# Output projection and second norm in token halves, two feed-forward operands placed between, output tiles that keep their slots

## The chip, the core and the metric

The kernel runs on one core of one Trainium2 chip. The metric is the device time of one execution in microseconds (us). Below, TensorE is the matrix engine (PE in the views, PEld its weight loads), VectorE is DVE, ScalarE is ACT, GpSimd is POOL, and SyncE (SP) issues the DMAs.

## The reference, cut to what matters

One layer of a streaming encoder for 1024 tokens of width 1024, in float32:

```
h   = rmsnorm(x, ln1)
mix = concat(pool_mixer, gla_mixer, forgetting_attention)(h @ w_in)   # 256 + 256 + 512 columns
x3  = x + mix @ w_o
h2  = rmsnorm(x3, ln2)
x4  = x3 + (silu(h2 @ w_gate) * (h2 @ w_up)) @ w_down                 # D_FF = 2816
out = rmsnorm(x4, ln_f)
```

The forgetting attention has eight heads of 64. It is causal, so a block of 256 queries m (0 to 3) looks at m + 1 blocks of 256 keys.

## The kernel before, in words

**Number format.** Each float32 operand is split into a high part (a copy into the matrix format, by ACT) and a low part (the difference, by VectorE or POOL). A product of two matrices is three matrix products: high x high, high x low, low x high.

**Stages.** Norm and projections; pooling and gated linear attention; four pairs of attention heads p = 0..3; output projection with the residual; second norm; gate and up projection (22 tiles fi of 128 columns); down projection; last norm. The feed-forward matrix products are done by a seven-product scheme on halves (products 1 to 7, in the order 3, 5, 4, 1, 2, 7, 6). So each needs operands that are sums of halves, split again into high and low.

**Output projection.** The mixed columns come as eight tiles mix0 to mix7 of 128 channels. `out_proj` makes a block tb of 128 tokens from four of them: first from mix0 to mix3 (PSUM name pxa), later from mix4 to mix7 (pxb), 24 products each, in two column halves; VectorE adds each to the residual tile xa (L576). Mix tiles are held in two groups g of 512 tokens. mix4 to mix6 are read back from DRAM as mr (L560), split by ACT (L562) and POOL (L563). mix7 is written in place by the last attention pair (`last_mix`). Before, group g holds the 256-token blocks g and g + 2, since tokens m * 256 go to `last_mix[m % 2]`. The last pair does its query blocks m in the order 3, 1, 2, 0, and pxb, x3d and the norm run over the blocks in the order 2, 3, 6, 7, 0, 1, 4, 5.

**Second norm.** For each block: ACT squares (L632), VectorE and POOL make the reciprocal root (n_v, n_r, L100 and L101), VectorE scales (L634), TensorE transposes (n2pt, L639), ACT copies to hr (L641). `left(i)` makes the left operand hA of product i from hr: a sum hs by VectorE where two halves are needed (L667), high by ACT (L670), low by VectorE (L671). hr0 and hr1 hold tokens 0 to 511, hr2 and hr3 tokens 512 to 1023. `right(fi)` loads wg and wu (L681, L682) and makes seven right operands: sum ws (L693; by POOL for the first two tiles), high (L694), low (L695). `gate_up` does the products m (L710).

**Slots.** SBUF is cut into 50 tiles of 128 x 1024 float32. `G` takes the first tile of a list `idle`, `free` puts one at its end, so that a new tile waits for whatever last used its slot. `ws` and some others come from a ring of two half tiles. PSUM has four tags: s (3 banks), pt (2), o (1), gm (2).

**Down projection.** `prep` makes the operands of two column tiles at a time: ra is loaded (L803), rw summed by POOL (L808), both split (L815 ACT, L816 VectorE) to ha, la, hw, lw. The last index is that of the first of the two tiles: rw6_10 is product 6, tile 10, a single one. The products d are at L916, their adds into the output tiles c at L894 and L896. `final(tb)` scales c (L883, L884), stores it to `out` and frees its slot.

**Order of instructions.** The program is written in the order of the functions, but a scheduler arranges the instructions of each engine by its own estimate of time. What an engine does in which order is therefore fixed when the kernel is built, and each engine works strictly in that order. So an edit in one place can move instructions in others.

Of the kernel before, what the change touches and what calls it, by code (L numbers as in the profile page):

```python
# [10 lines left out]
F32R = mybir.dt.float32r  # L11
I8 = mybir.dt.int8
AF = mybir.ActivationFunctionType
ALU = mybir.AluOpType
# [4 lines left out]
P = 128  # L19
NT = T // P  # L20
# [11 lines left out]
def tile_hybrid_block(ctx: ExitStack, tc, x, w_fv, w_gv, w_zt, w_o, w_gu, w_down, ln, w_pool, w_a3, chans, b_f, consts, out):  # L32
    nc = tc.nc
    ACT, DVE, POOL, PE, SP = nc.scalar, nc.vector, nc.gpsimd, nc.tensor, nc.sync
# [8 lines left out]
    idle = list(range(NSLOT))  # L43
    where = {}
    rings, n_ = {}, NSLOT
# [4 lines left out]
    def G(name, dtype=F32):  # L50
        i = idle.pop(0)
        t_ = big.tile([P, 1024], dtype, tag=f"g{i}", name=name)
        where[name] = i
        return t_

    def free(*names):
        for n in names:
            idle.append(where.pop(n))
# [10 lines left out]
    def f(ap):  # L69
        return ap.bitcast(F32)  # L70
# [181 lines left out]
    last_mix = []  # L252
# [205 lines left out]
    def fox_item(p, a, m, ops, fb, V):  # L458
# [6 lines left out]
        for i in range(2):  # L465
# [3 lines left out]
            w = W // nh  # L469
# [59 lines left out]
        if p < 3:  # L529
            SP.dma_start(mixd[4 + p, rows, m * 256:(m + 1) * 256], oy[rows])  # L530
        else:
            hi, lo = (last_mix[m % 2][rows, h, (m // 2) * 256:(m // 2 + 1) * 256] for h in range(2))
            ACT.activation(hi, oy[rows], AF.Copy)
            POOL.tensor_tensor(out=lo, in0=oy[rows], in1=f(hi), op=ALU.subtract)

    def fox_attend(p, ops, V):
        fbs = []
        for a in range(2):
            fb = R(f"fb{p}_{a}", tag="fb")
            SP.dma_start(fb, Fd[2 * p + a:2 * p + a + 1, :].broadcast_to([P, T]))  # L540
            fbs.append(fb)
        for a, m in ([(a, m) for a in range(2) for m in range(4)] if p < 3 else [(a, m) for m in (3, 1, 2, 0) for a in range(2)]):
            fox_item(p, a, m, ops, fbs[a], V)


# [2 lines left out]
    def load_mix(k0, g):  # L548

        mixes = []  # L550
        for k in range(k0, k0 + 4):
            if k == 7:
                mixes.append(last_mix[g])
                free(f"mr6_{g}")
                break
            if k % 2 == 0:
                raw = G(f"mr{k}_{g}").rearrange("p (k c t) -> p k c t", k=2, c=2)
            t_ = G(f"mix{k}_{g}", F32R).rearrange("p (h t) -> p h t", h=2)
            src = raw[:, k % 2]
            SP.dma_start(src, mixd[k].rearrange("p (c g t) -> p c g t", c=2, g=2)[:, :, g])  # L560
            hi, lo = (t_[:, h].rearrange("p (c t) -> p c t", c=2) for h in range(2))
            ACT.activation(hi, src, AF.Copy)  # L562
            POOL.tensor_tensor(out=lo, in0=src, in1=f(hi), op=ALU.subtract)  # L563
            mixes.append(t_)
            if k % 2:
                free(f"mr{k - 1}_{g}")
        return mixes

    def out_proj(tb, x2, mixes, ws, name):

        o0 = (tb // 4) * 256 + (tb % 2) * P
        for nh in range(2):
            ns = slice(nh * 512, nh * 512 + 512)
            ps = PS("gm", f"{name}{tb}_{nh}")
            gemm(ps, [((t_[:, 0, o0:o0 + P], t_[:, 1, o0:o0 + P]), (wh[:, ns], wl[:, ns])) for t_, (wh, wl) in zip(mixes, ws)])
            DVE.tensor_tensor(out=x2[:, ns], in0=ps, in1=x2[:, ns], op=ALU.add)  # L576
# [33 lines left out]
    xs = {}  # L610
    for g in range(2):
        mixes = load_mix(0, g)
        for tb in (2 * g, 2 * g + 1, 2 * g + 4, 2 * g + 5):
            xs[tb] = G(f"xa{tb}")
            SP.dma_start(xs[tb], x[tb * P:(tb + 1) * P, :])
            out_proj(tb, xs[tb], mixes, ws, "pxa")
        free(*[f"mix{k}_{g}" for k in range(4)])
# [11 lines left out]
    def norm2(tb, x2):  # L629
        ss = S(f"n2ss{tb}")  # L630
        sq = G(f"n2sq{tb}")
        ACT.activation(sq, x2, AF.Square, scale=D ** -0.5, accum_out=ss)  # L632
        r = rstd_D(ss, 1, f"n2{tb}")
        DVE.scalar_tensor_tensor(out=sq, in0=x2, scalar=r[:, 0:1], in1=ln2, op0=ALU.mult, op1=ALU.mult)  # L634
        o = slice((tb % 4) * P, (tb % 4) * P + P)
        for half in range(2):
            pt = PS("pt", f"n2pt{tb}_{half}")
            for k in range(4):
                PE.transpose(pt[:, k * P:(k + 1) * P], sq[:, (4 * half + k) * P:(4 * half + k + 1) * P], ident)  # L639
            for kp in range(2):  # L640
                ACT.activation(raw[2 * (tb // 4) + half][kp][:, :, o],  # L641
                               pt[:, 2 * kp * P:(2 * kp + 2) * P].rearrange("p (k t) -> p k t", k=2), AF.Copy)
        free(f"n2sq{tb}")

    mixes = [load_mix(4, g) for g in (1, 0)][::-1]
    for tb in (2, 3, 6, 7, 0, 1, 4, 5):
        g = (tb // 2) % 2
        out_proj(tb, xs[tb], mixes[g], ws, "pxb")
        SP.dma_start(x3d[tb], xs[tb])
        norm2(tb, xs[tb])  # L650
        free(f"xa{tb}")
        if tb in (7, 5):
            free(*[f"mix{k}_{g}" for k in range(4, 8)])
    free("wo6h", "wo6l", "wo7h", "wo7l", "ln2b")
    idle.extend(rings.pop("wr") + rings.pop("w"))


    hA = {}

    def left(i, in0, in1=None, op=None):  # L660
        hA[i] = []
        for kp in range(2):
            hi, lo = (G(f"hA{i}_{kp}{h}", F32R).rearrange("p (k t) -> p k t", k=2) for h in "hl")
            src = raw[in0][kp]
            if in1 is not None:
                t_ = G(f"hs{i}{kp}").rearrange("p (k t) -> p k t", k=2)
                DVE.tensor_tensor(out=t_, in0=src, in1=raw[in1][kp], op=op)  # L667
                src = t_
                free(f"hs{i}{kp}")
            ACT.activation(hi, src, AF.Copy)  # L670
            DVE.tensor_tensor(out=lo, in0=src, in1=f(hi), op=ALU.subtract)  # L671
            hA[i].append((hi, lo))


    cd = dpool.tile([7, NF // 2, P, 512], F32, name="cd")
# [114 lines left out]
    def prep(count):  # L790
        for i, j0, nj in items[len(ready):count]:
# [30 lines left out]
                    free(f"wd0_{j}", f"wd1_{j}")  # L822
            ready.append(ops)

    seen = []

    def start(fi):
        w_ = right(fi)

        def done(i):  # L830
            free(f"wr{fi}_{i}")
            if fi == NF - 1:
# [6 lines left out]

    lefts = {1: (0, 3, ALU.add), 4: (3,), 2: (2, 3, ALU.add), 3: (0,), 5: (0, 1, ALU.add), 7: (1, 3, ALU.subtract),  # L840
             6: (2, 0, ALU.subtract)}
    first = [start(fi) for fi in range(2)]
    for i in (3, 5, 4, 1, 2, 7, 6):
        left(i, *lefts[i])
        if i == 7:
            free("hr1_0", "hr1_1", "hr3_0", "hr3_1")
        for g_ in first:
            next(g_)
# [31 lines left out]
    def final(tb):  # L880
        x2 = cx[tb]
        r = rstd_D(sums[tb], 2, f"f{tb}")
        DVE.scalar_tensor_tensor(out=x2[:, 512:], in0=x2[:, 512:], scalar=r[:, 0:1], in1=lnf[:, 512:], op0=ALU.mult, op1=ALU.mult)  # L883
        ACT.activation(x2[:, 0:512], x2[:, 0:512], AF.Copy, scale=r[:, 0:1])  # L884
        for nh in (1, 0):
            ns = slice(nh * 512, nh * 512 + 512)
            SP.dma_start(out[tb * P:(tb + 1) * P, ns], x2[:, ns])
        free(f"c{tb}")

    def add_down(i, t, bank):  # L890
        for th, nh, sign in DEST[i]:
# [117 lines left out]
```

## Time and profile before

| | us |
|---|---|
| median of three runs | 1199.56 |
| lowest and highest | 1198.48, 1200.44 |
| profiled execution, its own time | 1203.56 |
| span of the profiled execution (first to last instruction) | 1201.8 |
| TensorE busy in the span | 1159.9 (97%) |
| VectorE busy | 810.2 (67%) |
| ACT busy | 530.9 (44%) |
| POOL busy | 390.9 (33%) |
| mean granted clock of TensorE | 0.979 |

Stages as the trace of before has them: last attention pair about 400 to 495 us, pxa beside it from 404 to 492, pxb and the second norm 498 to 561, gate and up 553 to 977, down projection 977 to 1195, last norm to 1201.8.

How to read the rows in the prediction. A row of the timeline has start, duration, engine, source line, operation, out<-in tile names, shape, and in brackets the idle time of the engine before it with what ended that. A row of a window has for each engine the busy time and the number of instructions, then the granted clock (PEclk), the share of the DMA engines, and GB/s. A row of the groups has the count, the busy time and the mean of one in ns, then idle time before. A row of the waits has the waiting operation, the one that released it, and us in total, times, longest. A row of the DMA issues has count, KB each, and the us from issue to landing. Line numbers are those of the kernel before. In the kernel after, the feed-forward functions stand above the pxb loop, so their lines differ: ws L664, high and low L665 and L666, m L681, rw L779, d L922.

### The profile page before, as it was taken

The numbers are of one execution on the slowest core, as the hardware profiler recorded it, in microseconds if no ns is written. First come the engines' busy times: TensorE is split into PE (matmuls) and PEld (weight loads), VectorE is DVE, ScalarE is ACT, GpSimd is POOL, SyncE is SP. The second block draws the span as 40 slices with busy tenths as digits, with TensorE's granted clock in tenths as the row PEclk, the third lists the DMA queues.
The fourth block names the chain that finished last, engine by engine and source line by source line (L and its number), as shares of the span: only waits on it lengthen the run. The fifth ranks groups of instructions, "written<-read, shape, count | busy, mean of one in ns | idle before, by whom it ended". The sixth has DMA issues, their size and how long they took to land.

```text
span 1201.8 us, 15933 instructions
## 1 busy us (share of the span) xinstructions
PE 1159.9 (97%) x5928; PEld 974.8 (81%) x5928; DVE 810.2 (67%) x1328; ACT 530.9 (44%) x965; POOL 390.9 (33%) x285
## 2 busy tenths in 40 slices
PE   6999999999999989899999999999999999999995
PEld 6878788889988778777888888888888888888874
DVE  7567612278748676468998768676776685766674
ACT  6362121257656745346444334443343344334353
POOL 2163122243333823331022220122202270660873
PEclk9999889899999999899999999999999999999998
DMA  6121111111122522221153331323224588333223
GB/s 244 35 71 53 54 35 53 36 55 47 47 62 77 169 91 97 79 105 53 53 155 112 111 120 65 131 93 118 95 90 148 214 322 288 109 96 118 63 97 140
DMA packets 53565, 126.34 MB, mean 105 GB/s; under 512 B 4792, under 2 KB 10344, under 8 KB 53488
## 3 DMA queue, kind: packets, MB, share of 16 engines
q1 hardware_dynamic: 53056, 123.75, 30.7%
q0 software_dynamic: 432, 1.57, 0.4%
q8 instruction: 46, 0.75, 0.3%
q14 instruction: 31, 0.25, 0.1%
HBM read 93.03 MB, written 32.28 MB: 104 GB/s over the span
## 4 chain that ended last, share of the span: by engine, by line
PE 84%; DVE 5%; DMA 3%; issue 3%; POOL 3%; ACT 2%; POOLq 0%; SPq 0%; ACTq 0%; DVEq 0%
PE m L710 35%; PE d L916 16%; PE pxa L138 4%; PE psv L138 3%; PE o L524 3%; PE pt L510 2%; PE s L484 1%; PE zq0p L138 1%; PE zgg0p L138 1%; PE s L485 1%; DMA mr<-mixd 1%; PE psg L138 1%; PE po L364 1%; PE zq3p L138 1%; PE zgg1p L138 1%
## 5 line engine op out<-in xcount | busy, mean ns | idle before, releaser
L710 PE MATMUL m<-hA_0h,wr 128*128 128x512 f32 x616 | 214.3, 390 | 0.6 <-ACT hr L641 0.5
L710 PE MATMUL m<-hA_1h,wr 128*128 128x512 f32 x616 | 214.6, 389 | 0.0
L710 PEld LDWEIGHTS m<-hA_0h,wr 128*128 128x128 f32 x616 | 115.6, 188 | 24.9 <-ACT hr L641 1.1
L710 PEld LDWEIGHTS m<-hA_1h,wr 128*128 128x128 f32 x616 | 115.7, 188 | 23.9
L916 PE MATMUL d<-hw,ha 128*128 128x512 f32 x308 | 120.0, 392 | 5.3 <-ACT hw L815 5.3
L710 PE MATMUL m<-hA_0l,wr 128*128 128x512 f32 x308 | 119.9, 389 | 1.7 <-DVE hA_0l L671 1.7
L916 PE MATMUL d<-lw,ha 128*128 128x512 f32 x308 | 120.4, 391 | 0.8 <-DVE lw L816 0.8
L710 PE MATMUL m<-hA_1l,wr 128*128 128x512 f32 x308 | 119.8, 389 | 0.0
L762 POOL TENSOR_TENSOR cg<-cu,cu 128x512 f32<-128x512 f32 x11 | 19.2, 1742 | 308.7 <-DVE cu L739 308.7
L916 PE MATMUL d<-hw,la 128*128 128x512 f32 x308 | 118.8, 391 | 0.0
L694 ACT ACTIVATE wr<-ws 128x512 fp32r<-128x512 f32 x110 | 69.5, 631 | 109.2 <-DVE ws L693 54.9
L695 DVE TENSOR_TENSOR wr<-ws,wr 128x512 fp32r<-128x512 f32 x110 | 75.9, 696 | 26.0 <-ACT wr L694 26.0
L816 DVE TENSOR_TENSOR la<-ra,ha 128x1024 fp32r<-128x1024 f32 (+1 forms) x42 | 58.2, 1392 | 29.0 <-ACT ha L815 21.5
L808 POOL TENSOR_TENSOR rw<-wd,wd 128x512 f32<-128x512 f32 x33 | 56.4, 1737 | 51.3 <-PE d L916 46.6
L916 PEld LDWEIGHTS d<-hw,ha 128*128 128x128 f32 x308 | 58.1, 189 | 17.8 <-ACT hw L815 5.7
L710 PEld LDWEIGHTS m<-hA_0l,wr 128*128 128x128 f32 x308 | 57.8, 188 | 14.2 <-DVE hA_0l L671 2.2
L916 PEld LDWEIGHTS d<-lw,ha 128*128 128x128 f32 x308 | 58.3, 189 | 13.3 <-DVE lw L816 1.2
L815 ACT ACTIVATE ha<-ra 128x1024 fp32r<-128x1024 f32 (+1 forms) x42 | 41.2, 987 | 61.6 <-DMA ra<-cd 56.0
L916 PEld LDWEIGHTS d<-hw,la 128*128 128x128 f32 x308 | 58.1, 189 | 12.1
L710 PEld LDWEIGHTS m<-hA_1l,wr 128*128 128x128 f32 x308 | 57.8, 188 | 12.1
L499 POOL TENSOR_TENSOR pb<-pb,rl 128x128 f32<-128x128 f32 (+3 forms) x32 | 38.1, 1196 | 83.4 <-DVE rl L496 66.5
L816 DVE TENSOR_TENSOR lw<-rw,hw 128x1024 fp32r<-128x1024 f32 (+1 forms) x30 | 45.7, 1535 | 27.3 <-ACT hw L815 27.2
(391 smaller groups left out, 2764.1 us busy)
## 6 DMA issues: line engine op xcount, KB each, us to landing
ra<-cd SPq DMA_DIRECT2D x35, 512.0 KB, 3.7
wu<-in_w_gu_dram SPq DMA_DIRECT2D x22, 512.0 KB, 4.3
wg<-in_w_gu_dram SPq DMA_DIRECT2D x22, 512.0 KB, 3.7
wd<-in_w_down_dram SPq DMA_DIRECT2D x22, 512.0 KB, 6.5
cd<-cg SPq DMA_DIRECT2D x11, 512.0 KB, 4.6
cd<-cs SPq DMA_DIRECT2D x11, 512.0 KB, 6.2
cd<-cu SPq DMA_DIRECT2D x11, 512.0 KB, 7.5
fb<-Fd SPq DMA_DIRECT2D x8, 512.0 KB, 4.5
```

Of the source, the lines that this page charges most:

```text
L138: PE.matmul(ps, a, b, start=(n == 0), stop=(n == last))
L499: POOL.tensor_tensor(out=pb[:, 0:W], in0=pb[:, 0:W], in1=rl[:, 0:1].broadcast_to([P, W]), op=ALU.mult)
L510: PE.transpose(pt[:, o0:o0 + P], Pb[i][:, (2 * n + b) * P:(2 * n + b + 1) * P], ident)
L524: PE.matmul(*args, start=(kb == 0 and n_ == 0), stop=(last and n_ == 1))
L694: ACT.activation(hi, src, AF.Copy)
L695: e2.tensor_tensor(out=lo, in0=src, in1=f(hi), op=ALU.subtract)
L710: PE.matmul(ps, a, b, start=(n == 0), stop=(n == 11))
L762: POOL.tensor_tensor(out=t_[:, 0:512], in0=a11, in1=a12, op=ALU.add)
L808: POOL.tensor_tensor(out=raw_[:, j * 512:j * 512 + 512], in0=wd[h0, j0 + j][:, e0, :], in1=wd[h1, j0 + j][:, e1, :], op=op)
L815: ACT.activation(hi[:, sl], src, AF.Copy)
L816: DVE.tensor_tensor(out=lo[:, sl], in0=src, in1=f(hi[:, sl]), op=ALU.subtract)
L916: PE.matmul(banks[t], a[:, o], b[:, ns], start=(j0 + j == 0 and m == 0), stop=(j0 + j == NF // 2 - 1 and m == 2))
```

## The change

- The last attention pair does its blocks m in the order 1, 0, 3, 2, and a group g holds the token half g (blocks 2g and 2g + 1). So a group's mr is loaded as one piece of 512 tokens.
- pxa, pxb, the stores x3d and the second norm run over tb = 0 to 7.
- Group 1 of mix4 to mix7 is asked for at tb = 2, and not ahead of the loop.
- At tb = 4, when tokens 0 to 511 are normed, the left operands of products 3 and 5 and the right operands of tile 0 are written; those of tile 1 follow behind the loop. For that the feed-forward functions stand ahead of the loop.
- `final` does not free the slot of c.

The core of the diff (the functions moved are the same text):

```diff
-            hi, lo = (last_mix[m % 2][rows, h, (m // 2) * 256:(m // 2 + 1) * 256] for h in range(2))
+            hi, lo = (last_mix[m // 2][rows, h, (m % 2) * 256:(m % 2 + 1) * 256] for h in range(2))
...
-        for a, m in ([(a, m) for a in range(2) for m in range(4)] if p < 3 else [(a, m) for m in (3, 1, 2, 0) for a in range(2)]):
+        for a, m in ([(a, m) for a in range(2) for m in range(4)] if p < 3 else [(a, m) for m in (1, 0, 3, 2) for a in range(2)]):
...
-                raw = G(f"mr{k}_{g}").rearrange("p (k c t) -> p k c t", k=2, c=2)
+                raw = G(f"mr{k}_{g}").rearrange("p (k t) -> p k t", k=2)
...
-            SP.dma_start(src, mixd[k].rearrange("p (c g t) -> p c g t", c=2, g=2)[:, :, g])
+            SP.dma_start(src, mixd[k, :, g * 512:(g + 1) * 512])
...
-        o0 = (tb // 4) * 256 + (tb % 2) * P
+        o0 = (tb % 4) * P
...
-        for tb in (2 * g, 2 * g + 1, 2 * g + 4, 2 * g + 5):
+        for tb in range(4 * g, 4 * g + 4):
...
-    mixes = [load_mix(4, g) for g in (1, 0)][::-1]
-    for tb in (2, 3, 6, 7, 0, 1, 4, 5):
-        g = (tb // 2) % 2
-        out_proj(tb, xs[tb], mixes[g], ws, "pxb")
-        SP.dma_start(x3d[tb], xs[tb])
-        norm2(tb, xs[tb])
-        free(f"xa{tb}")
-        if tb in (7, 5):
-            free(*[f"mix{k}_{g}" for k in range(4, 8)])
-    free("wo6h", "wo6l", "wo7h", "wo7l", "ln2b")
...
-    first = [start(fi) for fi in range(2)]
+    mixes = [load_mix(4, 0), None]
+    first = []
+    for tb in range(NT):
+        if tb == 2:
+            mixes[1] = load_mix(4, 1)
+        if tb == 4:
+            free(*[f"mix{k}_0" for k in range(4, 8)])
+            for i in (3, 5):
+                left(i, *lefts[i])
+            first.append(start(0))
+        out_proj(tb, xs[tb], mixes[tb // 4], ws, "pxb")
+        SP.dma_start(x3d[tb], xs[tb])
+        norm2(tb, xs[tb])
+        free(f"xa{tb}")
+    free("wo6h", "wo6l", "wo7h", "wo7l", "ln2b", *[f"mix{k}_1" for k in range(4, 8)])
+    idle.extend(rings.pop("wr") + rings.pop("w"))
+    first.append(start(1))
     for i in (3, 5, 4, 1, 2, 7, 6):
-        left(i, *lefts[i])
+        if i not in (3, 5):
+            left(i, *lefts[i])
...
-        free(f"c{tb}")
```

What the scheduler makes of it is seen in the order of each engine. First POOL near the end of the program, before: rw6_2 to rw6_10 are sums for the last products, c0 to c3 (L878) output tiles that are multiplied by the norm's weight, f0_r to f3_r their reciprocal roots.

```order
L808 TENSOR_TENSOR rw6_4_10183<-wd0_5_8906,wd1_5_8638 128x512
L808 TENSOR_TENSOR rw6_2_10102<-wd0_2_8847,wd1_2_8617 128x512
L808 TENSOR_TENSOR rw6_2_10102<-wd0_3_8849,wd1_3_8634 128x512
...
L878 TENSOR_TENSOR c3_8870<-c3_8870,lnfb_9255 128x512
L101 TENSOR_TENSOR f2_r_10153<-f2_v_10152,mhalf_76 128x1
L101 TENSOR_TENSOR f3_r_10166<-f3_v_10165,mhalf_76 128x1
L808 TENSOR_TENSOR rw6_10_10294<-wd0_10_9024,wd1_10_8678 128x512
L101 TENSOR_TENSOR f4_r_10318<-f4_v_10317,mhalf_76 128x1
```

The same place of POOL after the change (L779 is the line of rw, L885 that of c):

```order
L779 TENSOR_TENSOR rw6_4_10183<-wd0_5_8906,wd1_5_8638 128x512
L779 TENSOR_TENSOR rw6_10_10294<-wd0_10_9024,wd1_10_8678 128x512
L779 TENSOR_TENSOR rw6_2_10102<-wd0_2_8847,wd1_2_8617 128x512
L779 TENSOR_TENSOR rw6_2_10102<-wd0_3_8849,wd1_3_8634 128x512
...
L885 TENSOR_TENSOR c3_8870<-c3_8870,lnfb_9255 128x512
L101 TENSOR_TENSOR f2_r_10153<-f2_v_10152,mhalf_76 128x1
L101 TENSOR_TENSOR f3_r_10166<-f3_v_10165,mhalf_76 128x1
L101 TENSOR_TENSOR f4_r_10318<-f4_v_10317,mhalf_76 128x1
```

The sum rw6_10 moved from behind f3_r to ahead of rw6_2, fourteen places up.

Second TensorE where the output projection ends, before: pxb5_1 is the last column half of the last block, n2pt4 and n2pt5 are the transposes of the last two blocks in that order, m0_3 and m1_3 product 3 of the feed-forward tiles 0 and 1.

```order
L138 MATMUL pxb5_1_5325<-wo7h_4911,mix7_0_4102 128x512
L639 MATMUL n2pt4_0_5297<-ident_69,n2sq4_5290 128x128 x4
L639 MATMUL n2pt4_1_5304<-ident_69,n2sq4_5290 128x128 x4
L710 MATMUL m0_3_5445<-hA3_0h_5437,wr0_3_5367 128x512
L710 MATMUL m1_3_5460<-hA3_0h_5437,wr1_3_5404 128x512
L710 MATMUL m0_3_5445<-hA3_0l_5438,wr0_3_5367 128x512
...
L639 MATMUL n2pt5_0_5348<-ident_69,n2sq5_5341 128x128 x4
L639 MATMUL n2pt5_1_5355<-ident_69,n2sq5_5341 128x128 x4
L710 MATMUL m0_5_5487<-hA5_0h_5475,wr0_5_5372 128x512
```

The same place after the change, where block 7 is the last:

```order
L138 MATMUL pxb6_1_5332<-wo7h_4911,mix7_1_4103 128x512
L681 MATMUL m1_3_5472<-hA3_0h_5159,wr1_3_5424 128x512
...
L138 MATMUL pxb7_1_5383<-wo7l_4912,mix7_1_4103 128x512
L639 MATMUL n2pt5_0_5304<-ident_69,n2sq5_5297 128x128 x4
L639 MATMUL n2pt5_1_5311<-ident_69,n2sq5_5297 128x128 x4
L138 MATMUL pxb7_1_5383<-wo7h_4911,mix7_1_4103 128x512
L639 MATMUL n2pt6_0_5355<-ident_69,n2sq6_5348 128x128 x4
L639 MATMUL n2pt6_1_5362<-ident_69,n2sq6_5348 128x128 x4
L639 MATMUL n2pt7_0_5406<-ident_69,n2sq7_5399 128x128 x4
L639 MATMUL n2pt7_1_5413<-ident_69,n2sq7_5399 128x128 x4
L681 MATMUL m0_5_5487<-hA5_0h_5167,wr0_5_5188 128x512
```

All 24 products m_3 now stand ahead of the end of pxb, and the transposes of blocks 5, 6 and 7 stand together at its end.

More of the change, by code (lines that the diff above doesn't have):

```diff
@@ L556, in load_mix @@
             if k % 2 == 0:
-                raw = G(f"mr{k}_{g}").rearrange("p (k c t) -> p k c t", k=2, c=2)
+                raw = G(f"mr{k}_{g}").rearrange("p (k t) -> p k t", k=2)
             t_ = G(f"mix{k}_{g}", F32R).rearrange("p (h t) -> p h t", h=2)
             src = raw[:, k % 2]
-            SP.dma_start(src, mixd[k].rearrange("p (c g t) -> p c g t", c=2, g=2)[:, :, g])
-            hi, lo = (t_[:, h].rearrange("p (c t) -> p c t", c=2) for h in range(2))
+            SP.dma_start(src, mixd[k, :, g * 512:(g + 1) * 512])
+            hi, lo = t_[:, 0], t_[:, 1]
             ACT.activation(hi, src, AF.Copy)
@@ L643, in norm2 @@
         free(f"n2sq{tb}")
-    mixes = [load_mix(4, g) for g in (1, 0)][::-1]
-    for tb in (2, 3, 6, 7, 0, 1, 4, 5):
-        g = (tb // 2) % 2
-        out_proj(tb, xs[tb], mixes[g], ws, "pxb")
-        SP.dma_start(x3d[tb], xs[tb])
-        norm2(tb, xs[tb])
-        free(f"xa{tb}")
-        if tb in (7, 5):
-            free(*[f"mix{k}_{g}" for k in range(4, 8)])
-    free("wo6h", "wo6l", "wo7h", "wo7l", "ln2b")
[L655 to L672, printed above, removed]
     cd = dpool.tile([7, NF // 2, P, 512], F32, name="cd")
@@ L823, in prep, with left @@
             ready.append(ops)
+    hA = {}
+    def left(i, in0, in1=None, op=None):
+        hA[i] = []
+        for kp in range(2):
+            hi, lo = (G(f"hA{i}_{kp}{h}", F32R).rearrange("p (k t) -> p k t", k=2) for h in "hl")
+            src = raw[in0][kp]
+            if in1 is not None:
+                t_ = G(f"hs{i}{kp}").rearrange("p (k t) -> p k t", k=2)
+                DVE.tensor_tensor(out=t_, in0=src, in1=raw[in1][kp], op=op)
+                src = t_
+                free(f"hs{i}{kp}")
+            ACT.activation(hi, src, AF.Copy)
+            DVE.tensor_tensor(out=lo, in0=src, in1=f(hi), op=ALU.subtract)
+            hA[i].append((hi, lo))
     seen = []
```

## The prediction

> **What bounds the kernel now.** I read the page first, then busy time by stretch, then the list of what TensorE waited for in the attention part.
>
> ```profile
> span 1201.8 us, 15933 instructions
> PE 1159.9 (97%) x5928; PEld 974.8 (81%) x5928; DVE 810.2 (67%) x1328; ACT 530.9 (44%) x965; POOL 390.9 (33%) x285
> 400.00:440.00 40.00, 33.10 (x174) 27.53 (x173) 29.84 (x63) 26.55 (x50) 27.58 (x21) 0.91 0.44 143
> 440.00:492.00 52.00, 52.00 (x301) 45.27 (x299) 32.43 (x71) 21.47 (x47) 12.73 (x13) 1.00 0.22 74
> 498.00:553.00 55.00, 53.70 (x247) 43.56 (x248) 34.48 (x47) 28.46 (x62) 24.73 (x23) 0.95 0.28 101
> 553.00:561.00 8.00, 5.55 (x30) 4.01 (x28) 6.09 (x8) 5.15 (x13) 0.55 (x1) 1.00 0.17 68
> 600.00:1150.00 550.00, 550.00 (x2428) 455.58 (x2427) 398.79 (x556) 222.94 (x346) 169.34 (x107) 1.00 0.40 135
> 1177.00:1202.00 25.00, 12.43 (x48) 9.49 (x46) 9.22 (x17) 8.28 (x16) 4.91 (x7) 0.83 0.40 149
> PE s L484 <- DVE mn L489: 2.5, 2, 1.5
> PE o L524 <- DVE pp L513: 2.0, 1, 2.0
> ```
>
> TensorE is the bound: it is 97% busy, and from 600 to 1150 it never stops at full clock (550.00 of 550.00, PEclk 1.00). The change leaves every product in, so it can move time only where TensorE stands still or runs slow. Three such places lie beside the edits: the last attention pair (33.10 of 40.00 busy), the step from the output projection into the feed-forward part (about 3 us lost between 498 and 561), and the end (12.43 of 25.00). The whole span holds 41.9 us of idle TensorE; these three and their waits are what is at stake.
>
> **The end: slots kept.** The longest wait beside an edit is that of the last down-projection products.
>
> ```profile
> 1177.10 0.39 PE L916 MATMUL d<-hw,la 128*128 128x512 f32 x1
> ...
> 1177.78 0.39 PE L916 MATMUL d<-hw,la 128*128 128x512 f32 x1
> 1183.43 1.22 PE L916 MATMUL d<-hw,ha 128*128 128x512 f32 x2 [5.26 <-ACT hw L815]
> ...
> 1184.45 0.63 PE L916 MATMUL d<-lw,ha 128*128 128x512 f32 x1
> ...
> 1186.57 0.40 PE L916 MATMUL d<-lw,ha 128*128 128x512 f32 x1
> ...
> 1194.30 0.39 PE L916 MATMUL d<-hw,la 128*128 128x512 f32 x1
> 1181.45 1.26 POOL L808 TENSOR_TENSOR rw<-wd,wd 128x512 f32<-128x512 f32 x1 [3.45 <-DMA out_dram<-c]
> 1182.75 0.63 ACT L815 ACTIVATE hw<-rw 128x512 fp32r<-128x512 f32 x1 [3.19 <-POOL rw L808]
> 1183.41 0.69 DVE L816 TENSOR_TENSOR lw<-rw,hw 128x512 fp32r<-128x512 f32 x1 [3.46 <-ACT hw L815]
> 1155.81 5.04 POOL L808 TENSOR_TENSOR rw<-wd,wd 128x512 f32<-128x512 f32 x4 [1.16 <-DVE la L816]
> 1160.27 1.67 DVE L816 TENSOR_TENSOR la<-ra,ha 128x1024 fp32r<-128x1024 f32 x1 [4.54 <-ACT ha L815]
> ...
> 1170.43 2.19 DVE L816 TENSOR_TENSOR lw<-rw,hw 128x1024 fp32r<-128x1024 f32 x1
> ```
>
> Read it backwards: the products need hw, hw needs the sum rw, and rw stood 3.45 us until the stores of a finished c tile had landed, because its slot was that tile's. With c tiles kept, the order puts rw6_10 ahead of rw6_2, where nothing of c is waited for. POOL's sum costs 1.26 us, ACT's half tile 0.63 and VectorE's 0.69; they go to about 1156 to 1160, into the 1.16 us that POOL and the 4.54 us that VectorE idle there. If that cover were gone they would push the next operands by at most their sum, 2.6 us. What is late next is lw6_8 (1170.43, 2.19), which now has one more half tile, la6_10, ahead of it: it ends at 1172.62 + 0.69 = 1173.3. Its first product stands 54 from the end in the new order; with the last one at 1187.3, that is 1175.0. So 1.7 us are left, and I cost this at nothing.
>
> Now the size. The three pitches from 1177.10 to 1177.78 are 0.227 us each. Without the stall the product at 1183.43 would start at 1178.01: 5.42 us. Behind the stall the products from 1184.45 to 1186.57 come 0.42 us apart (five pitches in 2.12), and only then 0.227 again. From 1183.43 to 1194.30 the trace has 42 products: 41 pitches take 10.87 us, where 41 x 0.227 is 9.31, so 1.56 us more. The sum is **7.0 us** off. Its bounds are 5.3 (the wait alone) and 7.0. What follows the last product does not change.
>
> The Trainium skill ("TensorE: Matmul & The Clock Gate", Part 1) says that the array's clock is halved after an idle window of about 3.4 us and comes back after as long of work; the 0.42 us pitch for about 3 us agrees.
>
> **The last attention pair and the first output-projection half.** The item order (3,1,2,0) becomes (1,0,3,2). No product is added.
>
> ```profile
> PE pt L510 <- DVE pp L513: 1.4, 1, 1.4
> 491.96 5.85 DMA mr<-mixd
> 494.99 0.68 PE L524 MATMUL o<-pp,v 128*128 128x256 f32 x4 [1.04 <-DVE ot L528]
> 498.51 0.79 PE L138 MATMUL pxb<-wo4h,mix 128*128 128x512 f32 x1 [2.84 <-ACT mix L562]
> 499.10 0.63 PE L138 MATMUL pxb<-wo4l,mix 128*128 128x512 f32 x1
> ...
> 502.51 0.63 PE L138 MATMUL pxb<-wo5l,mix 128*128 128x512 f32 x1
> ```
>
> From 400 to 440 TensorE loses 6.9 us to the VectorE softmax chain, 2.5, 2.0 and 1.4 of it in the rows shown, and runs at 0.91. Now the two short items stand first: their VectorE work is smaller, so the previous pair's copies, for which TensorE waits here, come sooner. The bounds are 0 (the previous pair's own chain still ends last) and 6.9 plus what the clock took, 0.09 x 40 = 3.6. VectorE is 75% busy here and 62% in the next stretch, so the long items can be paid later. I take about half of the idle time, 3.3 us.
>
> Against it stands the wait for mr. Its slot still comes from the last pxa product, so 5.85 us of DMA and ACT's mix still follow it. Before, the last item's small products filled some of these 6.5 us; now three to five small groups of them have gone forward. They are worth about 0.7 us (the 0.68 row) plus transposes; I take 1.3 lost. The net is **2.0 us** off, with bounds +1.3 and -9.
>
> The group's loads are 128x512 in one piece instead of 128x2x256. That cannot move much beside a fixed 5.85 us; I cost it at 0.
>
> **Into the feed-forward part.** The 24 products m_3 now stand inside pxb6 and pxb7, but n2pt5 is put behind 11 products of pxb7_1, n2pt6 and n2pt7 behind the last, and m_5 behind those.
>
> ```profile
> 552.73 1.03 PE L639 MATMUL n2pt<-ident,n2sq 128*128 128x128 f32 x8
> 555.95 0.50 PE L710 MATMUL m<-hA_0l,wr 128*128 128x512 f32 x1 [1.72 <-DVE hA_0l L671]
> 560.78 1.05 PE L710 MATMUL m<-hA_0h,wr 128*128 128x512 f32 x2 [0.53 <-ACT hr L641]
> L634 DVE SCALAR_TENSOR_TENSOR n2sq<-xa,n_r,ln2b 128x1024 f32<-128x1024 f32 x8 | 11.9, 1492 | 3.9 <-POOL n_r L101 3.7
> L576 DVE TENSOR_TENSOR xa<-pxb,xa 128x512 f32<-128x512 f32 x16 | 10.8, 682 | 3.7 <-PE pxb L138 3.7
> L641 ACT ACTIVATE hr<-n2pt 128x256 f32<-128x256 f32 x32 | 9.6, 386 | 1.8 <-PE n2pt L639 1.8
> L632 ACT ACTIVATE n2sq<-xa 128x1024 f32<-128x1024 f32 x8 | 8.5, 1061 | 13.8 <-DVE xa L576 13.8
> L101 POOL TENSOR_TENSOR n_r<-n_v,mhalf 128x1 f32<-128x1 f32 x8 | 4.9, 610 | 18.8 <-DVE n_v L100 18.8
> L693 POOL TENSOR_TENSOR ws<-wg,wu 128x512 f32<-128x512 f32 x6 | 8.5, 1427 | 4.0 <-DVE wr L695 4.0
> L100 DVE TENSOR_SCALAR n_v<-n2ss 128x1 f32<-128x1 f32 x8 | 1.2, 152 | 6.1 <-ACT n2sq L632 6.1
> L695 DVE TENSOR_TENSOR wr<-ws,wr 128x512 fp32r<-128x512 f32 x10 | 8.0, 812 | 1.4 <-ACT wr L694 1.4
> wu<-in_w_gu_dram SPq DMA_DIRECT2D x22, 512.0 KB, 4.3
> ```
>
> Before, TensorE lost 55.00 - 53.70 = 1.3 us (0.5 of it ahead of the first pxb product) and 8.00 - 5.55 = 2.45 us here: 3.2. After, there is one hole: from the last pxb product TensorE must wait for the add (0.68), the square (1.06), n_v and n_r (0.15 and 0.61), and the scaling (1.49): 4.0, with hops between four engines 4.6, less some 0.8 us of n2pt6 that is done meanwhile (m's next product at 553.52 follows n2pt at 552.73): about 4. Filling it is not possible, as m_5 stands behind n2pt7 in TensorE's queue. Behind the hole the clock may be low: the hole of 2.84 + 1.04 us ahead of 498.51 was followed by some ten products 0.43 us apart (502.51 - 499.10 = 3.41 for eight), 2 us lost. A shorter hole, 1.72 at 555.95, was not. So the loss after is between 4 and 6 against 3.2, and half of the slow products would lie beside a wait for hA4's low part that comes either way: **1.5 us** on, with bounds -1 and +5.
>
> The same part of the Trainium skill speaks against this edit: by its window a hole of 4 us is always followed by half clock for 3.4 us, 1.7 us lost. By it alone the term would be 4 + 1.7 - 3.2 = 2.5 and the time 1193.0.
>
> Queues: ws1_1 (1.43) now stands ahead of n_r of blocks 5 and 6 on POOL, and wr1_7 on ACT stands ahead of the hr copies (0.39 each) of block 5. Both wait for VectorE. Between the last product of block 5 and its n2pt stand 71 products, 16 us, and its norm takes 4, so I cost them at nothing; without that cover they cost up to the 5 of the bound. The loads of wg0, wu0, wg1 and wu1 stand behind stores on SP. The first m_3 product stands behind 13 half groups of 12 products and five n2pt: 13 x 12 x 0.227 + 2 (slow start) + 5 x 0.8 = 41 us after the first pxb product, and m1_3 some 4 us later. wu1 stands behind wg1, which waits for POOL's ws0_6, and that for a difference freed by n2pt2: nine half groups and three n2pt, 9 x 12 x 0.227 + 2 + 2.4 = 29 us, then 0.81 + 1.43 + 4.3 for the load, about 36. Then ws1_3, wr1_3 (1.43, 0.63): 38, against 45.
>
> **The sum.** 7.0 + 2.0 - 1.5 = 7.5 us off. The profiled execution, 1203.56 us, becomes about 1196; its span lay 1.8 us under its time and it was 4.0 us over the median of the three runs. The same 7.5 off the median 1199.56 gives **1192.0 us**. Changes under 0.2% (2.4 us) can't be told from none here.
>
> **The rivals.**
> - The attention order fills nearly all of the 6.9 us, and the clock stays up: 5 us more, 1187. For it: VectorE has room in the next stretch. Against: the previous pair's chain is the same length. 0.17.
> - Only the wait goes at the end, or half of it, since lw6_8 or ra6_10 comes late: 2 to 3 us less, 1195. Against: 4.54 us of room. 0.08.
> - The hole is longer: the last square stands on ACT behind wr1_7 (0.63) and four hr copies (0.39 each), 2.2 us, and wr1_7 waits for POOL. 4 + 2.2 and 2 of slow clock against 3.2 is 5, 3.5 more than I took: 1195.5. For it: wr1_7's sum waits for VectorE. 0.12.
> - Slower: tile 1's right operands are late. m1_3 stands ahead of pxb7 in TensorE's queue, and wr1_3 needs wu1. If wu1 lands later than about 43 us after the first pxb product, each us is one more for all that follows, pxb7 and its norm with it. By the sum above it lands at 36, so it decides from 7 us late on, and takes 7.5 + 2.4 = 10 more, 17 us late, to give 1202. Six POOL sums of 1.43 and ten VectorE differences of 0.81 at twice their time could do it. 0.04.
> - The change doesn't do what it says at the end, because rw6_10's new slot waits too: it waits only for operations long done in the order, so 0.01, 1199.
>
> **How the numbers follow.** My case has 0.58, its own range 1190 to 1194. The range takes in the second, third and first rival and the bounds of the hole: 1186.5 to 1197.0. Faster by over 0.2% is all but the last two rivals and a rest of 0.04 where two of the small losses fall together: 0.91. Within 0.2%: 0.05; slower: 0.04.
>
> **What would show it.** Right: no TensorE wait over 1 us after 1150 but the 0.8 one for lw; products 0.23 us apart to the end; rw6_10 among the sums, not behind the f_r; busy in 400 to 440 well over 33.10; one hole of about 4 us ahead of n2pt7. Wrong: a wait for wr ahead of pxb7, a wait of some us for another operand near the end, or a first pxb product that comes no earlier than at 498.51.

## The result and the profile after

| | us | ratio to before (95% interval) |
|---|---|---|
| before, median of 10 runs | 1199.96 (1196.22 to 1203.84) | |
| after, median of 10 runs | 1194.09 (1191.04 to 1196.72) | 0.995 (0.9932 to 0.9967) |
| after, measured a second time beside later experiments | 1190.12 (1187.43 to 1191.71) | 0.9929 (0.9908 to 0.9949) |
| forecast | 1192.0 | 0.9937 |

By the two ratios the change makes the kernel 6 to 8.5 us faster. The profiled execution has 1191.04 us as its own time and 1189.1 as its span. The spans of the two traces differ by 12.7 us, and that is more than the change gave: 6.2 us of it come before the first product of zk3p, at 382.3 before and 376.1 after, where no edit is. The last section says what they are. So the traces are compared from that product on, in stretches between events that both kernels have.

| us between | before | after | difference | forecast |
|---|---|---|---|---|
| first zk3p product, first pxb product (attention) | 116.2 | 112.4 | -3.8 | -2.0 |
| to the last m product (the step, and gate and up) | 478.2 | 480.3 | +2.1 | +1.5 |
| to the last d product (down projection) | 217.6 | 210.7 | -6.9 | -7.0 |
| to the end of the span (closing) | 7.5 | 9.5 | +2.0 | 0 |
| sum (each row rounded by itself) | 819.5 | 813.0 | -6.5 | -7.5 |

The same places after, first the windows. The changed kernel is 6 us further on than before in the first of them and 8 to 10 in the others.

```profile
400.00:440.00 40.00, 34.97 (x199) 29.27 (x199) 33.81 (x75) 26.27 (x56) 23.49 (x20) 0.96 0.44 143
440.00:492.00 52.00, 49.16 (x272) 41.97 (x271) 25.54 (x49) 20.63 (x42) 16.57 (x16) 0.97 0.21 71
553.00:561.00 8.00, 8.00 (x29) 6.34 (x28) 6.68 (x7) 7.51 (x11) 0.00 (x0) 0.71 0.00 1
600.00:1150.00 550.00, 550.00 (x2429) 455.40 (x2427) 403.07 (x552) 222.80 (x343) 173.10 (x108) 1.00 0.40 134
```

The middle is as full as it was. From 553 to 561 TensorE is now busy all the time, but its clock is 0.71: that is no gain. From the list of its waits over the whole execution, the lines of these places:

```profile
PE n2pt L639 <- DVE n2sq L634: 3.1, 1, 3.1
PE pxb L138 <- ACT mix L562: 2.3, 1, 2.3
PE n2pt L639 <- ACT hr L641: 1.1, 1, 1.1
PE d L922 <- DVE lw L787: 0.9, 1, 0.9
PE m L681 <- DVE hA_0l L810: 0.3, 1, 0.3
```

The 5.3 us for hw are gone, nothing at the end has taken their place on TensorE, and no wait for wr is there. New are 3.1 and 1.1 us ahead of n2pt. The timeline of TensorE at that hole:

```profile
545.22 1.04 PE L639 MATMUL n2pt<-ident,n2sq 128*128 128x128 f32 x8
547.60 1.20 PE L639 MATMUL n2pt<-ident,n2sq 128*128 128x128 f32 x8 [1.10 <-ACT hr L641]
551.93 1.94 PE L639 MATMUL n2pt<-ident,n2sq 128*128 128x128 f32 x8 [3.13 <-DVE n2sq L634]
...
555.63 0.63 PE L681 MATMUL m<-hA_0l,wr 128*128 128x512 f32 x1
```

These are n2pt5, n2pt6 and n2pt7: 4.2 us of waiting in two pieces, and behind it eight transposes in 1.94 us where 1.04 is usual, then products of 0.63 us. The clock has fallen.

The end, on VectorE. Before the change the last scaling of c0 to c3 ends at 1178.93, two adds into the last tiles wait for their products, and only then comes the first scaling of such a tile:

```profile
1177.52 1.41 DVE L883 SCALAR_TENSOR_TENSOR c<-c,f_r,lnfb 128x512 f32<-128x512 f32 x2 [0.44 <-POOL f_r L101]
...
1186.39 0.69 DVE L894 TENSOR_TENSOR c<-d,c 128x512 f32<-128x512 f32 x1 [2.29 <-PE d L916]
1187.92 0.69 DVE L894 TENSOR_TENSOR c<-d,c 128x512 f32<-128x512 f32 x1 [0.84 <-PE d L916]
...
1189.53 0.74 DVE L883 SCALAR_TENSOR_TENSOR c<-c,f_r,lnfb 128x512 f32<-128x512 f32 x1
```

After the change: row by row the last four output tiles (L900 add, L100 root's first step, L890 scaling), and the last product on TensorE.

```profile
1169.14 1.78 DVE L890 SCALAR_TENSOR_TENSOR c<-c,f_r,lnfb 128x512 f32<-128x512 f32 x1 [1.44 <-POOL f_r L101]
1171.37 1.41 DVE L890 SCALAR_TENSOR_TENSOR c<-c,f_r,lnfb 128x512 f32<-128x512 f32 x2 [0.44 <-POOL f_r L101]
1172.70 0.68 DVE L900 TENSOR_TENSOR c<-d,c 128x512 f32<-128x512 f32 x1
1174.17 0.21 DVE L100 TENSOR_SCALAR f_v<-fss 128x1 f32<-128x1 f32 x1 [0.79 <-ACT d L880]
1175.05 0.75 DVE L890 SCALAR_TENSOR_TENSOR c<-c,f_r,lnfb 128x512 f32<-128x512 f32 x1 [0.66 <-POOL f_r L101]
1175.72 0.68 DVE L900 TENSOR_TENSOR c<-d,c 128x512 f32<-128x512 f32 x1
...
1178.74 0.68 DVE L900 TENSOR_TENSOR c<-d,c 128x512 f32<-128x512 f32 x1
...
1182.12 0.68 DVE L900 TENSOR_TENSOR c<-d,c 128x512 f32<-128x512 f32 x1
1183.59 0.21 DVE L100 TENSOR_SCALAR f_v<-fss 128x1 f32<-128x1 f32 x1 [0.79 <-ACT d L880]
1184.47 0.75 DVE L890 SCALAR_TENSOR_TENSOR c<-c,f_r,lnfb 128x512 f32<-128x512 f32 x1 [0.66 <-POOL f_r L101]
...
1179.57 0.39 PE L922 MATMUL d<-hw,la 128*128 128x512 f32 x1
```

TensorE is done at 1179.96, but the add into c7 comes at 1182.12. None of the four adds waits for a product (no releaser stands behind them). Each comes 3.0 us after the one ahead of it (the last 3.4), because the scaling of the tile before stands between them in VectorE's queue, and that waits for ACT's square and POOL's root. The row of L890 at 1169.14 takes 1.78 us beside POOL's multiplication of a tile by the norm's weight (L885), and 0.75 at 1175.05 without it.

### The profile page after: what moved, and what is told of

Same layout as the page of the kernel before. It is cut to its first block, busy times and chain, and to the rows that moved or that the text cites. A ratio compares the mean times of both kernels' runs of the same rounds, so it can differ in the third digit from the quotient of the medians.

```text
span 1189.1 us, 15922 instructions
## 1 busy us (share of the span) xinstructions
PE 1152.6 (97%) x5928; PEld 971.1 (82%) x5928; DVE 814.8 (69%) x1328; ACT 531.3 (45%) x965; POOL 394.9 (33%) x285
## 4 chain that ended last, share of the span: by engine, by line
PE 87%; DVE 4%; POOL 2%; DMA 2%; ACT 2%; issue 2%; SPq 0%; POOLq 0%; ACTq 0%; DVEq 0%
PE m L681 35%; PE d L922 15%; PE pxa L138 4%; PE psv L138 3%; PE o L524 3%; PE pxb L138 2%; PE pt L510 2%; PE psg L138 2%; PE s L484 1%; PE s L485 1%; PE zgg0p L138 1%; PE zq0p L138 1%; PE po L364 1%; PE zq3p L138 1%; PE zk3p L138 1%
## 5 line engine op out<-in xcount | busy, mean ns | idle before, releaser
L681 PEld LDWEIGHTS m<-hA_0h,wr 128*128 128x128 f32 x616 | 116.2, 189 | 24.4 <-ACT hr L641 0.3
L779 POOL TENSOR_TENSOR rw<-wd,wd 128x512 f32<-128x512 f32 x33 | 59.8, 1838 | 46.8 <-PE d L922 46.7
L787 DVE TENSOR_TENSOR lw<-rw,hw 128x1024 fp32r<-128x1024 f32 (+1 forms) x30 | 49.0, 1644 | 19.6 <-ACT hw L786 19.4
```

The source lines that it names most:

```text
L681: PE.matmul(ps, a, b, start=(n == 0), stop=(n == 11))
L779: POOL.tensor_tensor(out=raw_[:, j * 512:j * 512 + 512], in0=wd[h0, j0 + j][:, e0, :], in1=wd[h1, j0 + j][:, e1, :], op=op)
L787: DVE.tensor_tensor(out=lo[:, sl], in0=src, in1=f(hi[:, sl]), op=ALU.subtract)
```

## The experiments

After the traces my theory A was four separate terms: attention -3.8, step +2.0, slots -6.8 up to the last product, closing +2.0. The rivals stand with each run. Where a number is given as "attention", "step" and so on, it is the stretch of the table above in the trace of that run. Ratios are to the kernel before, run beside it on the same chip.

**E1. The changed kernel with the slots freed again.**

```diff
             SP.dma_start(out[tb * P:(tb + 1) * P, ns], x2[:, ns])
+        free(f"c{tb}")
```

> The changed kernel, but a finished output tile frees its slot again. Theory A (three separate terms, as the two traces read: slots -4.8 us, made of -6.8 until the last product and +2.0 behind it; attention part -3.8; step into the feed-forward part +2.0): about 1.8 us faster than the kernel before, so about 1198, and in its trace a TensorE wait of 5 us for hw near the end, the time from the last product to the end back at 7.5 us from 9.5. Rival B (all of the gain is the slots', attention and the step cancel or are run-to-run spread): the time of the kernel before, 1200, within 1 us.

Measured: ratio 0.9996 (0.9979 to 1.0014). The trace has its wait back, and 218.4 and 7.5 us in the last two stretches:

```profile
PE d L923 <- ACT hw L786: 5.1, 1, 5.1
```

Attention 111.7, step 479.6: together 3.2 us under before. The interval takes in both theory A's -1.8 us and rival B's 0. The whole time thus doesn't tell them apart; the slot term is shown.

**E2. The kernel before with the slots kept.**

```diff
-        free(f"c{tb}")
```

> The kernel before, with only the freeing of the output tiles' slots taken out. Theory A: 4.8 us faster than before, about 1195; in the trace no wait for hw near the end, products 0.23 us apart, and 9.5 us from the last product to the end. Rival B: 6 us or more faster, 1194 or less, with 7.5 us behind the last product. If slots alone do nothing, 1200.

Measured: ratio 0.9946 (0.9927 to 0.9965), some 6.5 us. The trace: down projection 210.6, closing 9.2. From the last m product to the end that is 219.9 where before has 225.1, so 5.2 us. The closing has grown here too, with no other edit in the kernel: the growth, some 2 us, belongs to the slots. The interval holds both 4.8 and 6 and more, but rival B's 7.5 us behind the last product was not there.

**E3. LAST = 4.** The last two pairs of column tiles are done block by block, not the last three.

```diff
-LAST = 3
+LAST = 4
```

> The changed kernel with LAST = 4 in place of 3: the last two pairs of column tiles, and not the last three, are done block by block at the end; the products are the same. In VectorE's order the add into c5 then stands ahead of the scaling of c4, where the changed kernel has it behind. Theory A (the 2.0 us that the end grew by are four round trips add, square, root, scale of 3.0 us each, one after another in VectorE's queue): 2 us faster than the changed kernel, about 1192, 7.5 us from the last product to the end. Rival C (the closing time grew for another reason, such as the stores or POOL's roots): no change, 1194.

Measured: ratio 0.9937 (0.9914 to 0.9959). Closing 8.4 in place of 9.5: 1.2 us off, not the 2.0 expected. VectorE's rows in this trace:

```profile
1172.56 0.69 DVE L900 TENSOR_TENSOR c<-d,c 128x512 f32<-128x512 f32 x1 [1.11 <-PE d L922]
...
1174.60 0.69 DVE L900 TENSOR_TENSOR c<-d,c 128x512 f32<-128x512 f32 x1 [0.34 <-PE d L922]
1175.21 0.74 DVE L890 SCALAR_TENSOR_TENSOR c<-c,f_r,lnfb 128x512 f32<-128x512 f32 x1
```

Now the first two adds wait for products (1.11 and 0.34 us), and the adds come 2.0 us apart. That VectorE's order set the end is shown by its turning round. The time of the whole kernel alone would not show it: the interval overlaps that of the changed kernel.

**E4. Other PSUM banks for m_5.** For the first two tiles.

```diff
-        m5 = m("pt", 5)
+        m5 = m("pt" if fi > 1 else ("o", "s")[fi], 5)
```

> The changed kernel, but product 5 of the first two feed-forward tiles takes other PSUM banks (o for tile 0, s for tile 1) than the transposes of the norm, so that it need not stand behind the transposes of block 7 in TensorE's queue; nothing else is edited. Theory A (the hole of 3.1 and 1.1 us in front of the last two transposes is there since the scheduler had nothing it could put in; the banks are why): the hole shrinks to 1 us or less and the slow products behind it go, 3 us faster than the changed kernel, about 1191. Rival D (the norm chain of blocks 5 to 7 and the left operands of product 4 behind it set the end of this part, whatever fills the hole): the wait moves to product 4's operands, no change, 1194.

Measured: ratio 0.9982 (0.9965 to 0.9999), by the ratios 4 to 6 us slower than the changed kernel (0.995 and 0.9929). The scheduler did move m_5 ahead of n2pt6 and n2pt7, as meant, and the hole there went. The waits of TensorE between 490 and 620 in this trace, and the window behind:

```profile
PE m L681 <- ACT hA_0h L809: 4.1, 2, 2.9
PE m L681 <- DVE hA_0l L810: 1.8, 1, 1.8
560.00:575.00 15.00, 10.51 (x28) 7.33 (x29) 14.46 (x14) 7.79 (x10) 0.00 (x0) 0.66 0.11 35
```

The hole has only gone behind: 5.9 us for the operands of product 4, at a clock of 0.66. The step is 483.4, 3.1 us longer than that of the changed kernel, so Rival D's "no change" missed too. Its mechanism fits the trace: the chain from the last pxb product through the norm of block 7 to hA4 sets when product 4 can start, and moving products forward only moves the hole. My theory A was wrong in naming the banks as the cause.

**E5. The operands behind the loop again,** slots kept, halves and item order as changed.

```diff
-            for i in (3, 5):
-                left(i, *lefts[i])
-            first.append(start(0))
...
-    first.append(start(1))
+    first += [start(0), start(1)]
     for i in (3, 5, 4, 1, 2, 7, 6):
-        if i not in (3, 5):
-            left(i, *lefts[i])
+        left(i, *lefts[i])
```

> The changed kernel, but the left operands of products 3 and 5 and the right operands of tile 0 are written behind the loop again, as before; slots kept, token halves and item order as changed. The scheduler then puts most of m_3 behind the transposes of block 6, where the hole is. Theory A (the step costs 2.0 us since m_3 was used up inside pxb, where TensorE had no gap to fill, and is missing behind the last pxb product): 2 us faster than the changed kernel, ratio to before about 0.993, and from the first pxb product to the last m product 478 us instead of 480.3. Rival E (the 2.0 us are the spread of one trace): as the changed kernel, ratio 0.995, 480.

Measured: ratio 0.9932 (0.9906 to 0.9957), 1188.72 us. Step 477.1. In this trace the waits of the step are short and apart: 1.3 us for hA_0l, at which m_3 stops, 1.1 for a mix tile, 0.7 each for wr and hr. The clock stays up in the last stretch of pxb and behind it:

```profile
544.94 0.50 PE L681 MATMUL m<-hA_0l,wr 128*128 128x512 f32 x1 [1.32 <-DVE hA_0l L810]
...
549.61 1.05 PE L681 MATMUL m<-hA_0h,wr 128*128 128x512 f32 x2 [0.74 <-ACT hr L641]
540.00:553.00 13.00, 10.89 (x53) 8.51 (x53) 10.20 (x11) 8.69 (x18) 0.55 (x1) 1.00 0.10 42
```

Against it, the same 13 us of the changed kernel:

```profile
540.00:553.00 13.00, 8.77 (x46) 7.17 (x45) 8.20 (x11) 7.67 (x18) 4.69 (x6) 0.91 0.20 81
```

10.89 us busy at full clock against 8.77 at 0.91. So the operands in between cost time; E9 and E10 repeat it. E6, below, has the operands in between too and a step of 478.5, with one wait of 2.1 us there, so the 2.9 to 3.2 us between these pairs hold for the new item order.

**E6. The old item order** (3, 1, 2, 0), all else as changed.

```diff
-        for a, m in ([(a, m) for a in range(2) for m in range(4)] if p < 3 else [(a, m) for m in (1, 0, 3, 2) for a in range(2)]):
+        for a, m in ([(a, m) for a in range(2) for m in range(4)] if p < 3 else [(a, m) for m in (3, 1, 2, 0) for a in range(2)]):
```

> The changed kernel, with the item order of the last attention pair as before (3, 1, 2, 0); token halves, operands and slots as changed. Theory A (the item order gives the 3.8 us between the last pair's projection and the first pxb product, since the short items first keep VectorE free for the pair before): 3 to 4 us slower than the changed kernel, ratio about 0.998, and from the first zk3p product to the first pxb product about 116 us instead of 112.5. Rival F (the token halves give it, as group 0 is ready early): no change, ratio 0.995, 112.5.

Measured: ratio 0.9967 (0.9948 to 0.9985). Attention 113.5, between 112.4 and 116.2. That looks as if order and halves gave half each, but the clock speaks against it. The stretch from the first zk3p product to the last pxa product, in the traces of before, after and E6:

```profile
382.32:491.54 109.22, 102.33 (x575) 0.97 0.30 99
376.14:483.20 107.06, 102.03 (x587) 0.98 0.30 98
378.89:485.09 106.20, 99.81 (x575) 1.00 0.31 99
```

(length, TensorE busy, clock, DMA share, GB/s.) TensorE idles 6.9 us before, 5.0 after and 6.4 in E6, so the old order has nearly the old idle time; E6 is short there because its clock never fell, where that of before stood at half for 3.4 us twice: the same 575 products keep TensorE busy for 99.8 us and not 102.3. Behind the last pxa product E6 takes 7.3 us to the first of pxb, as before (7.0), and not 5.4. So what can be seen is the part of the item order, 1.9 us against the mean of the ten traces that have it (111.6); that the halves alone give anything is not shown.

The sum of down projection and closing in E6 is 213.4 + 7.5 = 220.9, where the changed kernel has 210.7 + 9.5 = 220.2. Here a wait for lw took 2.1 us and not 0.9, the products ended later, and the end of the kernel did not move. That is once more VectorE's chain, not the last product.

**E7. Item order, halves and block order alone**: the edits of E1 and E5 together.

> The kernel before with the item order, the token halves and the block order 0 to 7 of the change alone: operands behind the loop, slots freed as before. Theory A: the attention part's 3.8 us and no loss at the step, so ratio to before 0.997, 1193.5 where before has 1197; a 5 us wait for hw stays at the end. Rival G (what is gained at the attention is lost in the step by the block order itself, with or without the operands in between): ratio 1.000.

Measured: ratio 0.9982 (0.996 to 1.0004), 2.2 us by the ratio. The trace: attention 110.4, step 477.0, down projection 218.5, closing 7.5, with its 5.3 us wait for hw. The interval holds 0.997 and 1.000, so the medians don't decide between theory A and rival G. The step of 477.0 speaks against G: no loss there without the operands in between.

**E8. LAST = 4 and the operands behind the loop.**

> The changed kernel with LAST = 4 and with the operands behind the loop, so the sum of two of the edits above. Theory A: 1.2 us (the shorter closing seen with LAST = 4) and 2.0 us (the step) under the changed kernel, ratio to before about 0.992, faster than the changed kernel (0.995) and than LAST = 4 alone (0.9937). If the step is a wash: 0.9937.

Measured: ratio 0.9937 (0.9916 to 0.9958). Step 477.6 and closing 8.1 came out; the median did not get under that of E5, and the 0.992 expected was missed. What LAST = 4 gives on top is not shown in the time.

**E9, E10, E11. Three kernels on one chip.** E9 is the changed kernel, E10 that of E5, E11 has in addition:

```diff
             square(t, 0, bank)
-            gain0(t)
             final(t)
...
-        ACT.activation(x2[:, 0:512], x2[:, 0:512], AF.Copy, scale=r[:, 0:1])
+        if tb < 4:
+            DVE.scalar_tensor_tensor(out=x2[:, 0:512], in0=x2[:, 0:512], scalar=r[:, 0:1], in1=lnf[:, 0:512], op0=ALU.mult, op1=ALU.mult)
+        else:
+            ACT.activation(x2[:, 0:512], x2[:, 0:512], AF.Copy, scale=r[:, 0:1])
```

> The changed kernel itself once more, beside the next two on one chip. By the terms of the traces so far (attention -4.2, step +2.6, slots until the last product -7.4, closing +1.9): 7 us faster than before, ratio 0.994; the first measurement gave 0.995.

> The changed kernel with the operands behind the loop, once more. By the terms: 2.6 us faster than the changed kernel beside it, ratio to before 0.992; from the first pxb product to the last m product 477 us where the changed kernel has 480. If the operands' place makes no difference: the same ratio as the changed kernel beside it.

> The kernel of the run before this, with one more edit: for output tiles 0 to 3 POOL's multiplication of the first half by the norm's weight is left out, and VectorE does it in the scaling of that half, in place of ACT. POOL's roots of tiles 1 to 3 then don't stand behind four sums of 1.3 to 1.8 us. Theory A (the end is set by four round trips in VectorE's queue, which start when tile 3 is scaled): the add into c4 starts about 1 us earlier counted from the last product, and the time from the last product to the end goes from 9.2 to about 8 us; 1 us faster. If four more scalings on VectorE (0.7 us each) fill what is gained: no change.

| | median us | ratio (interval) | attention | step | down | closing |
|---|---|---|---|---|---|---|
| E9 | 1190.12 | 0.9929 (0.9908 to 0.9949) | 111.2 | 479.8 | 210.6 | 9.5 |
| E10 | 1188.05 | 0.9915 (0.9897 to 0.9932) | 111.6 | 476.9 | 211.9 | 8.1 |
| E11 | 1188.48 | 0.9921 (0.9903 to 0.994) | 111.8 | 477.6 | 210.6 | 7.9 |

E10 is the kernel with the lowest median here; beside the changed kernel it is 2.1 us faster by the medians, as the step's 2.9 us would have it, though the intervals overlap. E11's chain on VectorE starts earlier: its add into c4 stands at 1169.33, 8.3 us ahead of the last product's start at 1177.6; in the changed kernel it was 6.9 (1172.70 to 1179.57). The closing is 7.9 against E5's 9.2, but the whole is not faster than E10, whose lw wait and closing fell out otherwise. So the 1 us is seen in the trace and not in the time.

**The terms over all traces.**

| stretch | with the edit | without |
|---|---|---|
| attention | 110.4 to 112.4 (ten traces) | 116.2, 115.4 (old item order and halves); 113.5 (E6) |
| step | 479.6, 479.8, 479.9, 480.3 (operands inside; E6 478.5 and E4 483.4 have other edits) | 476.8 to 478.2 (seven) |
| down and closing | 219.8 to 220.9 (slots kept, seven), 218.5 to 219.0 (E3, E8, E11) | 225.1, 225.9, 226.0 |

The means give attention -4.2, step +2.6, slots -5.5 with the closing in them: -7.1 us, a ratio of 0.994, between the two that were measured. With E6 counted among the steps with the operands inside, that term is +2.3. The attention term is the weakest: it rests on two traces without the edit, in which the clock took more (4.1 and 2.7 us, summed over its records) than in any of the ten (0 to 2.4), and in the time of the whole kernel E7, with the attention edits and the block order, shows 2.2 us (-0.5 to 4.8).

## Why the prediction was right, point by point

**The whole** came out within the range, at 0.995 and 0.9929 around the forecast 0.9937. By the pair of traces two errors of the terms took each other out: the attention gave 1.8 us more than forecast, and the closing took 2.0 that had been put at nothing. That the sum came so near is luck.

**The end until the last product** was right: 6.9 us for a forecast of 7.0, in the stall and in the slow products behind it. The three small steps made no later operand late: the lw wait stays (0.9). They did not go where the prediction put them: VectorE's came at 1147.79, among POOL's sums, and took 1.78 us, not 0.69. E1 and E2 show it from both sides.

**"What follows the last product does not change" failed**, and cost 2.0 us. I had read the closing of before as fixed. But there the stall had covered VectorE's work: it was done with c0 to c3 at 1178.93, 15.4 us ahead of the last product, and the scheduler had put two adds ahead of the first scaling. With the stall gone, it is done with them at 1172.78, 6.8 us ahead of the last product, and these scalings, held by POOL's multiplications and roots, stand right ahead of the add into c4. d6_0's last product is 45 from the end, so it was there by 1179.57 - 45 x 0.227 = 1169.4; the add came at 1172.70. From then the end was four round trips away. I had asked what is late next of the operands only, and not of the results. E2 shows that it comes with the slots, E3 that it is VectorE's order.

**The attention part** had the right sign and about half the size. From the first zk3p product to the last pxa product it went from 109.2 us (382.3 to 491.54) to 107.1 (376.1 to 483.20): 2.2, for 3.3 - 1.3 = 2.0 forecast. That agreement is in part luck: the idle time fell by 1.9 us and not by 3.3, and the clock stood at half for 3.4 us twice in this stretch before and once after; E2, with the old order, has one such fall too.

The rest is a step that failed: the prediction takes the load of mr as "a fixed 5.85 us". From the last pxa product to the first of pxb it took 6.97 us before and 5.37 after, since the load of mr was shorter. The chain of after:

```profile
483.62 4.25 DMA mr<-mixd
```

Around it (485 to 500 us before, 478 to 490 after) the same bytes go in 433 packets and not 689, the 1 KB packets being 2 KB now. In two pieces the load took 5.85 (before) and 5.65 us (E2), in one piece 4.12 to 4.40 in the ten traces with the new item order. But E6, in one piece with the old order, took 6.14, and an earlier load of mr, some 40 us behind the first zk3p product, took 4.33 (before) and 3.78 us (E2) in two pieces and 3.81 to 4.42 in one. So the shape alone is not the cause. What the three slow loads share is the old item order, and with it the place of another load of 512 KB, that of ln2b. Issues in before, after and E6:

```profile
491.32 0.65 POOL L626 DMA_DIRECT2D ln2b<-in_ln_dram  x1
491.96 1.17 SPq L560 DMA_DIRECT2D mr<-mixd  x2
```

```profile
482.54 0.65 POOL L626 DMA_DIRECT2D ln2b<-in_ln_dram  x1 [0.61 <-PE pxa L138]
483.62 0.80 SPq L560 DMA_DIRECT2D mr<-mixd  x2
```

```profile
484.87 0.65 POOL L626 DMA_DIRECT2D ln2b<-in_ln_dram  x1
485.51 0.80 SPq L560 DMA_DIRECT2D mr<-mixd  x2
```

ln2b was asked for 0.64 us ahead of mr in the three slow cases (E2 too) and 1.08 us ahead in the ten quick ones. That it held mr up is likely and not shown, as no run moves ln2b alone.

**The step** was right: 1.5 forecast, 2.1 in the pair of traces, 2.3 to 2.6 over all. By the prediction's own figures (4 us, half of 2, less 3.2) the term would have been 1.8. The hole was 4.2 us for "about 4", and eight transposes and some eight products behind it ran slow. I had taken half of that as hidden; nearly none was. The 2.5 us worked out from the Trainium skill ("TensorE: Matmul & The Clock Gate", Part 1) was nearer than my term. That the operands' loads and POOL's order cost nothing was right: no wait for wr is in the list.

**The rivals.** That the attention fills everything: no, 3.8 to 4.2 us in all where it took 7. That only half of the end's wait goes: no. That the hole costs 5: no. The slower case, tile 1's operand late: no sign of it. None had the closing in it.

## What to carry to other kernels

When a stall is taken out, ask whose work it covered: here VectorE's scaling of four tiles lay beside it, and 2 of the 7 us came back as a chain of its own. Work that can be done early is worth most where the engine is going to wait, so don't use up what could lie beside the last block's norm to fill a place that has no gap. And compare two traces from an event ahead of the edit, in stretches, since their whole spans may differ by more than the edit is worth.

## What the runs showed of the hardware that was not expected

The 6.2 us ahead of every edit are the clock. Its mean up to the first zk3p product is 0.96 over 382.3 us before and 0.98 over 376.1 us after; summed over the clock's records that is 13.7 and 6.8 us lost. From 165 us on it falls there while TensorE has no idle time at all. Windows of before, then of after:

```profile
210.00:220.00 10.00, 10.00 (x38) 7.85 (x38) 0.87 (x3) 0.98 (x2) 0.08 (x1) 0.64 0.00 0
```

```profile
200.00:210.00 10.00, 10.00 (x59) 7.86 (x59) 2.22 (x5) 0.77 (x2) 1.64 (x1) 0.66 0.04 14
210.00:220.00 10.00, 10.00 (x60) 8.11 (x59) 2.99 (x5) 1.57 (x3) 1.37 (x1) 1.00 0.00 0
```

TensorE is busy 10.00 of 10.00 us in all three, at 0.64, 0.66 and 1.00. The fall stands in both traces, earlier and shorter after (6.8 us at half clock, 10.2 before). Ahead of it stand many small products, with 64 columns or from 64 rows. In the following rows of before the same two groups take 0.43 and 0.33 us ahead of the fall, at 206.9, and 0.69 and 0.48 behind it.

```profile
205.52 0.43 PE L364 MATMUL po<-gv,attb 128*128 128x64 f32 x2
205.89 0.33 PE L368 MATMUL po<-St,bc 64*64 64x64 f32 x4
206.15 1.41 PE L353 MATMUL pat<-eq,d 64*128 64x128 f32 x8
207.48 0.69 PE L364 MATMUL po<-gv,attb 128*128 128x64 f32 x2
208.10 0.48 PE L368 MATMUL po<-St,bc 64*64 64x64 f32 x4
```

The Trainium skill ("TensorE: Matmul & The Clock Gate", Part 1) has the clock fall after an idle window; in these rows there is no idle time, so small products seem to count as little work, which no run here tries. In the traces of before and after each fall, up to the last product, is to half clock and lasts 3.4 us or a multiple of it. Elsewhere it also comes behind single waits of 1.4 and 2.0 us (before, at 408.3 and 425.4), while in E6 the clock stayed up behind one of 2.0. How long the clock is down ahead of zk3p differs from one execution to the next, and so does the time: of the ten runs of the changed kernel the fastest, 1191.04 us, has a mean clock of 0.986, and the slowest, 1196.72 us, 0.982. The start of zk3p lies between 376.1 and 382.5 us in all traces here, whatever the kernel.
